# Modulation sums traced one group of products later in a two-layer trunk

## The chip, the core and the metric

The kernel runs on one core of a Trainium2 chip. The metric is the device time of one execution in microseconds (us); for the kernel before there are three runs, and their median counts.

## What is computed

A trunk of two layers acts on `x` (256 tokens x 1024). Each layer has three sub-layers, six in all, each wrapped in a modulation that depends on one conditioning vector `c`:

```python
def adaln_sublayer(x, m, f, ln_g, ln_b):
    shift, scale, gate = m[:, None, 0], m[:, None, 1], m[:, None, 2]
    y = f(x * (1 + scale) + shift)
    return layer_norm(DEEPNORM_ALPHA * x + (1 + gate) * y, ln_g, ln_b)
...
    cs = jax.nn.silu(c)
    for layer in range(DEPTH):
        mod = (cs @ mod_w[layer] + mod_b[layer]).reshape(bsz, N_SUB, 3, D_MODEL)
```

So each sub-layer needs three vectors of 1024 (scale and shift before `f`, the gate behind it), each `cs` (1024) times a 1024 x 1024 block of `mod_w`: 18 such products, 4 MB of weights each. `f` is a SwiGLU with d_ff 2816 (sub-layers 0, 2, 3, 5: ffn0 to ffn3), a hybrid of sparse attention and gated DeltaNet (sub-layer 1), and latent attention (MLA, sub-layer 4). All products are in float32.

## The kernel before

Large products are made of three passes on TensorE (`mm3`, L261; its instructions are L263 to L265), for which weights and activations are split into two parts: a cast on ACT (L258) and a subtraction on DVE or POOL (L259).

**An ffn** (L411) has 11 chunks of 256 columns. For chunk c, PE does the 96 gate and up products into four PSUM banks (pool tag `gu`, all four of them), then the 24 down products that belong to chunk c-1, then chunk c+1. ACT takes the SiLU of the gate (L548), DVE multiplies with the up part (`sg`, L551, the last reader of two banks) and splits the result (`h`). The last five down rows are kept for the end: there PE goes through the four accumulators one after the other with 15 products each. This is called the tail here; the epilogue (L381 and on: gate, residual, norm) follows it bank by bank. Down weights are loaded in tiles of 512 KB, pool tag `wd`, three slots.

**The modulation** is a background generator, `mod_gen` (L185). It does not use PE for the products: a tile of `mod_w` (128 x 1024, tag `wd` as well, so the same three slots) is multiplied on DVE with the column of `cs` that belongs to its partitions and added into `macc` (L218 for the first, L225 for the other seven tiles of a set). Behind the eighth, the 128 partitions are summed in `mod_sums` (L236): for scale and shift `mod_cols` transposes `macc` in eight pieces on PE (L138) into two banks, which DVE reduces (L139); for the gate `mod_gate` multiplies by a matrix of ones (L180, two products of 512 columns) and DVE adds the banks to `G` (L182). Sets come in the order scale, shift, gate of each sub-layer. There is one `macc`, so the first step of a set waits until the sums of the set before have read it.

**The order.** `pace` (L55) pulls as many steps as the progress of the sub-layer asks for; an ffn calls it twice in each chunk, traced behind the chunk's gate and up products and ahead of the down products. In the hybrid it is called by `beat` (L927) at fixed points, in the MLA once a head. `need` (L252) pulls a set to its end on demand, at the end of a sub-layer. The loads, all issued by SP in one order, the steps and the sums thus get their places; a scheduler then sets the final order of each engine from the traced one, and `behind` (L110) keeps an instruction from being ordered ahead of a given one on its own engine. PE, DVE and SP each work through their order strictly. The four places of a chunk:

```python
                        self.pace(max(0, i + 1 - skip) / (NT - 2 - skip))
                next(self.rest, None)
...
                if c:
                    for i in range(2 * c - 2, min(2 * c, NT - L)):
                        down(i, every)
```

Of the kernel before, what the change touches and what calls it, by code (L numbers as in the profile page):

```python
# [33 lines left out]
class Trunk:  # L34
# [20 lines left out]
    def pace(self, part):  # L55

        goal = self.base + math.ceil((self.goal - self.base) * min(part, 1.0))
        while self.count < goal:
            self.count += next(self.bg)
        if part > 1.0:  # L60
            self.need(self.si, 2)
            if self.si + 1 < len(self.subs):
                self.need(self.si + 1, 0)
# [121 lines left out]
    def mod_gen(self):  # L185
# [4 lines left out]
        ws, loaded, G, step = {}, 0, None, None  # L190
# [14 lines left out]
        for n, (si, i, k) in enumerate(todo):  # L205
            if k == 0:
                l, j = self.subs[si]
                off = (j * 3 + i) * D
                acc = self.tl(self.wp, [P, D], "G", bufs=2) if si == 0 and i < 2 else self.tl(self.wp, [P, D], "macc")
                if i == 2:  # L210
                    G = self.tl(self.wp, [P, D], "G", bufs=2)
# [12 lines left out]
            else:  # L224
                step = nc.vector.scalar_tensor_tensor(acc, w, c, acc, ALU.mult, ALU.add)  # L225
            yield 1
            if k < KD - 1:
                continue
            self.mod_sums(si, i, acc, G, step)
            self.mdone.add((si, i))  # L230
            yield 0
            if si == 0 and i == 1:
# [606 lines left out]
    def run(self, subs):  # L839
# [1 line left out]
        self.subs = subs  # L841
        self.mdone = set()
        self.count = 0
        self.marks, self.last_mm = [None], None
        self.left = None
        goals = (44, 64, 98, 132, 136, 144)
        self.setup()
# [690 lines left out]
```

## Time and profile before

| what | us |
|---|---|
| median of 3 runs | 1210.27 |
| lowest and highest run | 1207.26, 1211.66 |
| the profiled execution | 1209.47 |
| its span in the trace | 1207.7 |

The profile is of one execution; times below are from the start of its span. Sub-layers lie about so: ffn0 to 224 us, hybrid to 475, ffn1 to 674, ffn2 to 886, MLA to 1003, ffn3 to the end. A chunk of an ffn takes some 17 us. In a timeline row the first number is the start, the second the duration, then engine, line, operation, and in brackets what the engine waited for before it and how long. Matmuls overlap, so a product with a duration of 0.28 or 0.39 us starts 0.12 or 0.23 us behind the one before it.

### The profile page before, as it was taken

How to read it: one execution, taken by the hardware profiler on the slowest of the kernel's cores; microseconds unless marked ns; L12 is line 12 of the kernel's file. 1: busy time of each engine (PE TensorE's matmuls, PEld its weight loads, DVE VectorE, ACT ScalarE, POOL GpSimd, SP SyncE). 2: the span in 40 equal slices, each digit the busy share in tenths (PEclk: the TensorE clock that was granted, in tenths of full speed). 3: DMA queues.
4: the chain of work that ended last, by engine and by line, in shares of the span. 5: the costliest groups of instructions: out<-in, count | busy, mean ns of one | idle time of the engine just before them, and what ended most of it. 6: DMA issues, size and time to landing. Idle time of an engine off the chain costs nothing.

```text
span 1207.7 us, 19560 instructions
## 1 busy us (share of the span) xinstructions
PE 1131.0 (94%) x7703; PEld 1025.9 (85%) x7703; DVE 917.7 (76%) x1404; ACT 548.5 (45%) x963; POOL 259.4 (21%) x186
## 2 busy tenths in 40 slices
PE   4998999998899998999999999999989998999997
PEld 3887999788787887989999899898988877899995
DVE  6699777698986677878775889767789748866545
ACT  0645444456433445543543543434347656544430
POOL 0631000224731452320000342000122234300001
PEclk9998999999999999999999899999989999999999
DMA  9879998453310576789987488888733335885620
GB/s 354 266 252 342 299 327 299 139 179 119 97 36 5 188 270 218 238 293 320 311 298 248 134 284 283 270 278 298 250 122 102 139 105 190 294 253 185 211 71 35
DMA packets 155333, 259.74 MB, mean 215 GB/s; under 512 B 8813, under 2 KB 117354, under 8 KB 155242
## 3 DMA queue, kind: packets, MB, share of 16 engines
q1 hardware_dynamic: 155050, 258.45, 64.4%
q8 instruction: 60, 0.98, 0.3%
q14 instruction: 31, 0.25, 0.1%
q10 hardware_dynamic: 192, 0.05, 0.0%
HBM read 257.43 MB, written 1.05 MB: 214 GB/s over the span
## 4 chain that ended last, share of the span: by engine, by line
PE 51%; DVE 23%; DMA 13%; issue 5%; ACT 4%; POOL 3%; SPq 0%; POOLq 0%; DVEq 0%; ACTq 0%
PE gu L265 8%; PE gu L263 8%; PE gu L264 8%; PE acc L265 6%; PE acc L264 6%; PE acc L263 6%; DMA wd<-ffn_w_down 5%; DMA wd<-mod_w 4%; DVE macc L225 3%; DMA w<-ffn_w_up 2%; DVE g L259 2%; DVE x L383 1%; POOL hd L259 1%; DMA w<-mod_w 1%; DVE u L259 1%
## 5 line engine op out<-in xcount | busy, mean ns | idle before, releaser
L225 DVE SCALAR_TENSOR_TENSOR macc<-wd,csT,macc 128x1024 f32<-128x1024 f32 x112 | 171.5, 1531 | 28.6 <-DMA wd<-mod_w 28.0
L265 PE MATMUL gu<-uT,g 128*128 128x256 f32 x640 | 181.3, 283 | 1.6 <-DVE g L259 1.6
L263 PE MATMUL gu<-uT,g 128*128 128x256 f32 x640 | 181.2, 283 | 1.3 <-ACT sg L548 1.3
L265 PE MATMUL gu<-uT,u 128*128 128x256 f32 x640 | 181.3, 283 | 1.0 <-DVE u L259 1.0
L263 PE MATMUL gu<-uT,u 128*128 128x256 f32 x640 | 181.2, 283 | 0.0
L264 PE MATMUL gu<-uT,u 128*128 128x256 f32 x640 | 181.1, 283 | 0.0
L264 PE MATMUL gu<-uT,g 128*128 128x256 f32 x640 | 181.1, 283 | 0.0
L258 ACT CAST hd<-wd 128x1024 fp32r<-128x1024 f32 x88 | 92.3, 1049 | 136.8 <-DMA wd<-ffn_w_down 118.8
L263 PE MATMUL acc<-hd,h 128*128 128x512 f32 x352 | 141.5, 402 | 0.5 <-ACT h L258 0.5
L265 PE MATMUL acc<-hd,h 128*128 128x512 f32 x352 | 138.0, 392 | 1.8 <-DVE h L259 1.8
L264 PE MATMUL acc<-hd,h 128*128 128x512 f32 x352 | 138.1, 392 | 0.0
L259 DVE TENSOR_TENSOR g<-w,g 128x1024 fp32r<-128x1024 f32 x86 | 117.0, 1364 | 23.9 <-ACT g L258 23.8
L263 PEld LDWEIGHTS gu<-uT,g 128*128 128x128 f32 x640 | 122.7, 192 | 3.2 <-ACT sg L548 1.8
L265 PEld LDWEIGHTS gu<-uT,g 128*128 128x128 f32 x640 | 122.7, 192 | 2.2 <-DVE g L259 2.2
L264 PEld LDWEIGHTS gu<-uT,g 128*128 128x128 f32 x640 | 122.7, 192 | 1.4
L265 PEld LDWEIGHTS gu<-uT,u 128*128 128x128 f32 x640 | 122.9, 192 | 1.2 <-DVE u L259 1.2
L264 PEld LDWEIGHTS gu<-uT,u 128*128 128x128 f32 x640 | 122.9, 192 | 0.0
L263 PEld LDWEIGHTS gu<-uT,u 128*128 128x128 f32 x640 | 122.9, 192 | 0.0
L259 DVE TENSOR_TENSOR u<-w,u 128x1024 fp32r<-128x1024 f32 x81 | 106.6, 1321 | 20.1 <-ACT u L258 20.0
L259 POOL TENSOR_TENSOR hd<-wd,hd 128x1024 fp32r<-128x1024 f32 x32 | 89.6, 2806 | 137.9 <-ACT hd L258 137.9
L258 ACT CAST u<-w 128x1024 fp32r<-128x1024 f32 (+1 forms) x89 | 91.7, 1038 | 58.1 <-DMA w<-ffn_w_up 44.8
L259 POOL TENSOR_TENSOR hl<-w,hl 128x1024 fp32r<-128x1024 f32 x28 | 72.5, 2602 | 202.0 <-ACT hl L258 201.5
(403 smaller groups left out, 2477.6 us busy)
## 6 DMA issues: line engine op xcount, KB each, us to landing
wd<-mod_w SPq DMA_DIRECT2D x130, 512.0 KB, 4.8
wd<-ffn_w_down SPq DMA_DIRECT2D x88, 512.0 KB, 4.6
w<-ffn_w_gate SPq DMA_DIRECT2D x43, 1024.0 KB, 8.4
w<-ffn_w_up SPq DMA_DIRECT2D x43, 1024.0 KB, 6.3
w<-hyb_w_in SPq DMA_DIRECT2D x16, 1024.0 KB, 6.1
w<-mod_w SPq DMA_DIRECT2D x7, 1024.0 KB, 7.5
w<-hyb_w_out SPq DMA_DIRECT2D x4, 1024.0 KB, 5.0
w<-mla_w_out SPq DMA_DIRECT2D x4, 1024.0 KB, 5.1
```

The lines of the kernel that those rows point to most:

```text
L225: step = nc.vector.scalar_tensor_tensor(acc, w, c, acc, ALU.mult, ALU.add)
L258: i = self.nc.scalar.copy(hi, src)
L259: return i, (eng or self.nc.vector).tensor_tensor(out=lo, in0=src, in1=hi.bitcast(F32), op=ALU.subtract)
L263: nc.tensor.matmul(out, lh, rh, start=first, stop=False)
L264: nc.tensor.matmul(out, lh, rl, start=False, stop=False)
L265: self.last_mm = nc.tensor.matmul(out, ll, rh, start=False, stop=last)
L383: V.tensor_tensor(out=x[:, b, sl], in0=tmp, in1=x[:, b, sl], op=ALU.add)
```

## The change

Behind the eighth step of a set, `mod_gen` no longer traces the sums at once. It notes the last product that was traced (`last_mm`, set by every `mm3`), gives control back, and `pace` pulls nothing more as long as no further product has been traced. The next call of `pace` that finds a new one resumes: the sums are traced, ordered behind the last product on PE, and the steps that were due meanwhile follow at once. `need` does not look at the mark and pulls the sums directly. The first sets of sub-layer 0 are made before any product and keep their place. Tiles, pools, the split of work over engines and the goals stay as they were.

```diff
--- before.py
+++ after.py
@@ -55,7 +55,8 @@
     def pace(self, part):
 
         goal = self.base + math.ceil((self.goal - self.base) * min(part, 1.0))
-        while self.count < goal:
+        while self.count < goal and (self.held is None or self.held is not self.last_mm):
+            self.held = None
             self.count += next(self.bg)
         if part > 1.0:
             self.need(self.si, 2)
@@ -226,7 +227,14 @@
             yield 1
             if k < KD - 1:
                 continue
-            self.mod_sums(si, i, acc, G, step)
+            if self.last_mm is not None:
+
+                self.held = self.last_mm
+                yield 0
+                with self.behind(self.last_mm):
+                    self.mod_sums(si, i, acc, G, step)
+            else:
+                self.mod_sums(si, i, acc, G, step)
             self.mdone.add((si, i))
             yield 0
             if si == 0 and i == 1:
@@ -841,7 +849,7 @@
         self.subs = subs
         self.mdone = set()
         self.count = 0
-        self.marks, self.last_mm = [None], None
+        self.marks, self.last_mm, self.held = [None], None, None
         self.left = None
         goals = (44, 64, 98, 132, 136, 144)
         self.setup()
```

Lines behind the first hunk shift by 1, behind the second by 8 (L180 is L181, L225 is L226, L259 is L267, L551 is L559).

**PE, first gate sum (ffn0).** `macc_75` is the gate set of sub-layer 0, `gu_116` the last bank of chunk 3's products, `gu_138` that of chunk 4's in the new order. Before:

```order
L264 MATMUL gu_116_798<-uT_15_124,u_112_792 128x256
L265 MATMUL gu_116_798<-uT_15_124,u_112_792 128x256
L180 MATMUL gu_128_926<-macc_75_505,one_72 128x512
L180 MATMUL gu_129_929<-macc_75_505,one_72 128x512
L263 MATMUL acc_81_528<-hd_98_680,h_96_675 128x512
L264 MATMUL acc_81_528<-hd_98_680,h_96_675 128x512
L265 MATMUL acc_81_528<-hd_98_680,h_96_675 128x512
L263 MATMUL acc_82_532<-hd_98_680,h_96_675 128x512
```

Now:

```order
L272 MATMUL gu_138_999<-uT_15_124,u_134_993 128x256
L273 MATMUL gu_138_999<-uT_15_124,u_134_993 128x256
L181 MATMUL gu_143_1107<-macc_75_505,one_72 128x512
L181 MATMUL gu_144_1110<-macc_75_505,one_72 128x512
L655 MATMUL gu_154_1170<-ident_67,fr_1137 128x128
L271 MATMUL acc_81_528<-hd_120_903,h_118_898 128x512
L272 MATMUL acc_81_528<-hd_120_903,h_118_898 128x512
L273 MATMUL acc_81_528<-hd_120_903,h_118_898 128x512
```

The two products of the sum stand behind the products of the next chunk and ahead of the down products that follow those; with them comes a transpose of the position tables.

**SP, last heads of the hybrid.** `hyb_w_out` is the out projection's weight, the `wd` tiles belong to the scale set of sub-layer 2. Before:

```order
L892 DMA w8_698_4446<-hyb_w_out 128x2x1024
L892 DMA w8_718_4531<-hyb_w_out 128x2x1024
L198 DMA wd_630_4080<-mod_w 128x1024
L198 DMA wd_636_4103<-mod_w 128x1024
L198 DMA wd_637_4106<-mod_w 128x1024
L198 DMA wd_643_4129<-mod_w 128x1024
L198 DMA wd_649_4152<-mod_w 128x1024
L892 DMA w8_727_4586<-hyb_w_out 128x2x1024
L198 DMA wd_655_4215<-mod_w 128x1024
L198 DMA wd_656_4218<-mod_w 128x1024
```

Now:

```order
L900 DMA w8_698_4446<-hyb_w_out 128x2x1024
L900 DMA w8_718_4531<-hyb_w_out 128x2x1024
L900 DMA w8_727_4586<-hyb_w_out 128x2x1024
L199 DMA wd_650_4200<-mod_w 128x1024
L199 DMA wd_651_4203<-mod_w 128x1024
L199 DMA wd_652_4206<-mod_w 128x1024
L199 DMA wd_653_4209<-mod_w 128x1024
L199 DMA wd_654_4212<-mod_w 128x1024
L199 DMA wd_655_4215<-mod_w 128x1024
L199 DMA wd_656_4218<-mod_w 128x1024
```

The third `hyb_w_out` tile now stands ahead of the modulation tiles, which follow it in one row; before, five of them were ahead of it. On DVE the steps for which they are loaded (`macc_648`, behind the gate's two additions L183) now stand in one row as well, ahead of the reduces of their own sum:

```order
L183 SCALAR_TENSOR_TENSOR G_265_2067<-gu_646_4190,G_265_2067 128x512
L183 SCALAR_TENSOR_TENSOR G_265_2067<-gu_647_4193,G_265_2067 128x512
L219 TENSOR_SCALAR macc_648_4196<-wd_612_3982,csT_79 128x1024
L763 TENSOR_TENSOR PT_689_4415<-gu_619_4048,sums_620_4049 128x512
L226 SCALAR_TENSOR_TENSOR macc_648_4196<-wd_618_4045,csT_79,macc_648_4196 128x1024
L226 SCALAR_TENSOR_TENSOR macc_648_4196<-wd_649_4197,csT_79,macc_648_4196 128x1024
L226 SCALAR_TENSOR_TENSOR macc_648_4196<-wd_650_4200,csT_79,macc_648_4196 128x1024
L226 SCALAR_TENSOR_TENSOR macc_648_4196<-wd_651_4203,csT_79,macc_648_4196 128x1024
L226 SCALAR_TENSOR_TENSOR macc_648_4196<-wd_652_4206,csT_79,macc_648_4196 128x1024
L226 SCALAR_TENSOR_TENSOR macc_648_4196<-wd_653_4209,csT_79,macc_648_4196 128x1024
L226 SCALAR_TENSOR_TENSOR macc_648_4196<-wd_654_4212,csT_79,macc_648_4196 128x1024
L140 TENSOR_REDUCE ms_667_4341<-gu_668_4342 128x4
```

Before, the steps of this set stood one by one between the L736 of the heads (L744 in the new lines).

**DVE, end of ffn2.** `sg` and `h` are the last activations of the ffn, `hd` the last down weights, `big` weights of the MLA, `macc_1276` and `macc_1290` the shift set of the MLA. Before:

```order
L225 SCALAR_TENSOR_TENSOR macc_1276_8461<-wd_1423_9387,csT_79,macc_1276_8461 128x1024
L259 TENSOR_TENSOR h_1295_8625<-sg_1294_8622,h_1295_8625 128x256
L225 SCALAR_TENSOR_TENSOR macc_1276_8461<-wd_1424_9389,csT_79,macc_1276_8461 128x1024
L259 TENSOR_TENSOR hd_1317_8785<-wd_1316_8783,hd_1317_8785 128x1024
L225 SCALAR_TENSOR_TENSOR macc_1276_8461<-wd_1443_9476,csT_79,macc_1276_8461 128x1024
L551 TENSOR_TENSOR sg_1309_8764<-gu_1306_8665,sg_1309_8764 128x256
L259 TENSOR_TENSOR h_1310_8767<-sg_1309_8764,h_1310_8767 128x256
L551 TENSOR_TENSOR sg_1313_8775<-gu_1308_8667,sg_1313_8775 128x256
L259 TENSOR_TENSOR big_1319_8859<-w8_1318_8857,big_1319_8859 128x672
L259 TENSOR_TENSOR h_1315_8780<-sg_1313_8775,h_1315_8780 128x256
L259 TENSOR_TENSOR big_1321_8866<-w8_1320_8864,big_1321_8866 128x672
L381 SCALAR_TENSOR_TENSOR tmp_1328_8889<-acc_1110_7203,G_958_6178 128x512
```

Now:

```order
L267 TENSOR_TENSOR hd_1317_8785<-wd_1316_8783,hd_1317_8785 128x1024
L226 SCALAR_TENSOR_TENSOR macc_1290_8612<-wd_1422_9385,csT_79,macc_1290_8612 128x1024
L226 SCALAR_TENSOR_TENSOR macc_1290_8612<-wd_1423_9387,csT_79,macc_1290_8612 128x1024
L559 TENSOR_TENSOR sg_1313_8775<-gu_1308_8667,sg_1313_8775 128x256
L267 TENSOR_TENSOR big_1319_8859<-w8_1318_8857,big_1319_8859 128x672
L267 TENSOR_TENSOR big_1321_8866<-w8_1320_8864,big_1321_8866 128x672
L267 TENSOR_TENSOR h_1315_8780<-sg_1313_8775,h_1315_8780 128x256
L226 SCALAR_TENSOR_TENSOR macc_1290_8612<-wd_1424_9389,csT_79,macc_1290_8612 128x1024
L267 TENSOR_TENSOR big_1323_8873<-w8_1322_8871,big_1323_8873 128x672
L389 SCALAR_TENSOR_TENSOR tmp_1328_8889<-acc_1103_7181,G_976_6340 128x512
L226 SCALAR_TENSOR_TENSOR macc_1290_8612<-wd_1443_9476,csT_79,macc_1290_8612 128x1024
```

The steps of 1422 and 1423 stand behind the last `hd` and directly ahead of the last `sg`, and those of 1424 and 1443 behind the last `h`, among the epilogue's first operations; before, all four stood ahead of the last two `sg`. The end of ffn0 has the same shape.

## Rows read from the trace of the kernel before

**Rows 1.** The page: engines' busy time (us, share of span, instructions) and the chain that ended last.

```profile
PE 1131.0 (94%) x7703; PEld 1025.9 (85%) x7703; DVE 917.7 (76%) x1404; ACT 548.5 (45%) x963; POOL 259.4 (21%) x186
...
PE 51%; DVE 23%; DMA 13%; issue 5%; ACT 4%; POOL 3%; SPq 0%; POOLq 0%; DVEq 0%; ACTq 0%
```

**Rows 2.** The view of tile macc: the steps (minimum, median, maximum ns), and idle time of its users.

```profile
L225 DVE SCALAR_TENSOR_TENSOR macc<-wd,csT,macc x112: 1268/1279/3430, 60.3 to 1128.2; 128x1024 f32<-128x1024 f32 x112
...
  DVE macc L225: 7.2, 3
```

**Rows 3.** Waits of PE over the whole span: total us, times, longest us.

```profile
PE gu L138 <- DVE sg L551: 3.2, 2, 2.4
```

**Rows 4.** Timeline of PE: start us, duration, line, operation, in brackets the wait before it.

```profile
97.92 3.75 PE L180 MATMUL gu<-macc,one 128*128 128x512 f32 x4 [4.18 <-DVE macc L225]
...
102.75 0.39 PE L263 MATMUL acc<-hd,h 128*128 128x512 f32 x1
...
522.39 1.96 PE L180 MATMUL gu<-macc,one 128*128 128x512 f32 x4 [0.94 <-DVE macc L225]
...
524.88 0.40 PE L263 MATMUL acc<-hd,h 128*128 128x512 f32 x1
...
762.87 0.66 PE L138 MATMUL gu<-ident,macc 128*128 128x128 f32 x4 [2.43 <-DVE sg L551]
...
835.28 0.63 PE L138 MATMUL gu<-ident,macc 128*128 128x128 f32 x4 [2.08 <-DVE macc L225]
...
837.42 0.78 PE L263 MATMUL acc<-hd,h 128*128 128x512 f32 x1
...
840.09 0.40 PE L263 MATMUL acc<-hd,h 128*128 128x512 f32 x1
840.32 0.40 PE L264 MATMUL acc<-hd,h 128*128 128x512 f32 x1
```

**Rows 5.** Stretches of PE: span, us, PE busy (instructions), granted clock, DMA share, GB/s.

```profile
98.00:102.00 4.00, 4.00 (x6) 0.50 1.09 373
...
763.00:767.00 4.00, 4.00 (x20) 1.00 1.01 352
...
837.00:840.00 3.00, 3.00 (x10) 0.50 0.87 283
```

**Rows 6.** Timelines of DVE and PE at the start of ffn0's chunk 4.

```profile
100.33 1.23 DVE L259 TENSOR_TENSOR g<-w,g 128x1024 fp32r<-128x1024 f32 x1 [1.32 <-ACT g L258]
...
107.77 0.28 PE L265 MATMUL gu<-uT,g 128*128 128x256 f32 x1
```

**Rows 7.** The page: DMA issues (KB, median us to landing), and the cast of a down weight.

```profile
L258 ACT CAST hd<-wd 128x1024 fp32r<-128x1024 f32 x88 | 92.3, 1049 | 136.8 <-DMA wd<-ffn_w_down 118.8
...
wd<-mod_w SPq DMA_DIRECT2D x130, 512.0 KB, 4.8
```

**Rows 8.** Timeline of DVE at the end of ffn0.

```profile
213.54 3.97 DVE L225 SCALAR_TENSOR_TENSOR macc<-wd,csT,macc 128x1024 f32<-128x1024 f32 x3 [2.21 <-DMA wd<-mod_w]
...
220.60 0.42 DVE L551 TENSOR_TENSOR sg<-gu,sg 128x256 f32<-128x256 f32 x1 [1.86 <-PE gu L265]
```

**Rows 9.** Timelines of PE and SP in the hybrid's last heads.

```profile
427.51 0.28 PE L265 MATMUL acc<-uT,hl 128*128 128x256 f32 x1
427.63 1.03 PE L138 MATMUL gu<-ident,macc 128*128 128x128 f32 x8
...
406.31 11.43 SPq L198 DMA_DIRECT2D wd<-mod_w  x5
...
423.64 0.38 SPq L892 DMA_DIRECT2D w<-hyb_w_out  x1
```

**Rows 10.** Timeline of DVE at the end of ffn2.

```profile
862.70 1.29 DVE L225 SCALAR_TENSOR_TENSOR macc<-wd,csT,macc 128x1024 f32<-128x1024 f32 x1 [2.39 <-DMA wd<-mod_w]
...
870.63 0.42 DVE L551 TENSOR_TENSOR sg<-gu,sg 128x256 f32<-128x256 f32 x1
871.28 0.86 DVE L259 TENSOR_TENSOR big<-w,big 128x672 fp32r<-128x672 f32 x1 [0.22 <-ACT big L258]
```

## Prediction

> **What bounds the kernel.** I read the engines' busy time first, then the chain that ended last, the waits of PE, the timelines of PE, DVE and SP around the sums, and the granted clock in those stretches. PE is busy 94% of the span and DVE 76%; the chain lies 51% on PE, 23% on DVE and 13% on DMA [rows 1]. So a microsecond counts only where PE stands still, and the change can gain only from places where PE waits for a modulation sum. The view of tile `macc` finds three such waits, 7.2 us in all [rows 2]. In the waits of PE stand two more at the transposes, 3.2 us, for `sg` L551: the operation that frees a PSUM bank, not the sum's own data [rows 3].
>
> **What the waits cost, with the clock.** PE's timeline places the three at 97.92 (4.18 us, a gate sum), 522.39 (0.94, a gate sum) and 835.28 (2.08, transposes) [rows 4]. The first and the last cost more than their length. After the wait before 97.92 the granted clock stands at 0.50 over 98 to 102 us, the lower level of 1.2 GHz; PE had been idle for the 4.18 us before [rows 5]. The gate sum with three products takes 102.75 - 97.92 = 4.83 us there, against 524.88 - 522.39 = 2.49 us at the full clock: 2.34 us lost. After 835.28 the clock is 0.50 over 837 to 840: six products take 840.09 - 837.42 = 2.67 us, against 6 x 0.23 (840.09 to 840.32) = 1.38: 1.29 lost [rows 4, 5]. I book 2.3 and 1.2. The possible gain is 7.2 + 3.5 = 10.7 us.
>
> **How much of it goes.** In the new order each of these sums stands a whole chunk (some 17 us) behind its last step, so the step is done; no sum before was ever later than 4.2 us. But at 97.92 another wait is close behind. Chunk 4 begins on PE at 107.77 and its first weights were split from 100.33 on, when their load had just landed [rows 6]. Without the wait PE is there at 97.92 - 4.18 + 24 x 0.23 = 99.3. In the new order one 512 KB load less stands ahead of those weights, so I put the split's end at 100.2: 0.9 us of new wait. **Gain: 10.7 - 0.9 = 9.8 us** (ends 7 and 11). The sums themselves, about 2 us of PE for a gate [rows 4] and 1 us for eight transposes [rows 9], are moved and not added. The two bank waits (3.2 us) may go or come at any sum; I count 0, with -3 and +3 as ends.
>
> **What the pause costs inside an ffn.** The steps that were held back come in a bunch of up to six, 1.27 us each, behind the next chunk's products. The weights of the later chunks are split over 10 us before their use, so I count 0. If that cover were gone, the price would be the loads: 4.8 us to landing for each mod_w tile, through three slots that the down weights share [rows 2, 7]. What follows comes from there, at the three places where a bunch meets the end of a part.
>
> **End of ffn0.** The shift sum of sub-layer 1 moves from behind chunk 8 to behind chunk 9. Let X be PE's arrival there. The gate set's first step writes the same `macc`, so it ends near X + 3.4; two slots later the last down weight of the tail lands (4.8 us each, plus cast 1.05 [rows 7] and split 1.23 [rows 6]), split at X + 16.5; the next two steps end at X + 19.1 and now stand ahead of the last `sg` on DVE; `sg` and `h` bring the last `h` to X + 20.4. PE reaches the tail at X + 15.3 (transposes 1.0, 12 products of 0.23, 96 of 0.12) and that `h` four weight rows of 0.69 later, X + 18.1. Before, three steps in a row began at 213.54 and ended by 217.5, and `sg` at 220.60 waited for nothing but PE [rows 8]. New stall 2.3 us by this count, 1 if loads land sooner; I take 1.9, and 0.6 for the two steps that now stand in the epilogue. **+2.5** (0 to 4).
>
> **Hybrid.** The gate sum of sub-layer 1 moves from ahead of the attention to its last heads, some 20 us later, about 421 to 423 us of the trace before. The seven steps behind it then stand in a row on DVE. Before, five of their loads were issued from 406.31 on, and the transposes at 427.63, 0.12 us behind the product before them, waited for nothing [rows 9]. Now the loads stand in SP's queue behind the third hyb_w_out tile, which was issued at 423.64. The first of the seven ends near 425.3 and frees a slot; +4.8 is 430.1, +4.8 after the step that uses it 436.2, and the last of them 437.5. PE, less delayed, comes to the transposes 86 products of 0.12 us after the sum, about 433.5. That is 4 us by 4.8 a load; I take 3.5. A wait nearly as long cost 2.3 us of clock at 97.92, so I add 2.0. **+5.5** (1 to 8).
>
> The Trainium skill bears on this price: DMA: Bandwidth & Descriptors, sections "Latency and other measured facts" and "Measured (HBM→SBUF, 128 partitions, SWDGE, issued from GpSimd)", gives about 2 us of fixed cost and 341 GB/s for 1 MB. By that an estimate for a lone 512 KB load is 2 + 1.5 = 3.5 us, two loads in a row end 2.6 us sooner, the hybrid would cost about 1 us, and the sum below would come to about -2 us. The row says 4.8 [rows 7], and it decides.
>
> **End of ffn1.** Its gate sum moves behind chunk 10; the last down weight and `h` come just in time by the same count. **+0.5** (0 to 1.5).
>
> **End of ffn2.** The scale sum of the MLA moves behind chunk 9, as at ffn0, with one step more. On DVE two steps, then `sg`, two splits of `big` (0.86 each) and one `h` follow; that `h` comes at X + 22.2 by the same reckoning, needed at X + 18.1. Before, a step waited for its load until 862.70 (2.39 us) and all were done before the tail; `sg` came at 870.63 and the first `big` at 871.28 [rows 10]. The stall is 4.1 us with loads of 4.8, about 2 with quicker ones: I take 3. Two more steps (2.5 us) now lie beside the epilogue's first operations; most of that is beside PE's last three banks, so 0.8. **+3.8** (1 to 8 with a clock fall).
>
> MLA and ffn3 keep their order but for names: 0. **Sum: -9.8 + 2.5 + 5.5 + 0.5 + 3.8 = +2.5 us**, made against the profiled execution of 1209.47 us (span 1207.7): 1212.0. The median of the runs shown is 0.8 above it, so 1212.8, and I say 1213.
>
> **Rivals.** *A, the queues catch up (faster).* The waits and clock losses go, and the loads land early enough at all three ends. For it: 2.39 us of waiting for a load hid before the tail of ffn2 [rows 10]. Against: the slots allow three loads at a time, whatever DMA could do. It leaves -9.8 + 0.5 + 0.6 + 0.8 = -7.9: 1202.4 as a median, down to 1200.
>
> *B, each new stall also takes the clock (slower).* One mechanism, at the ends of ffn0 and ffn2: PE stops for `h` with products of three banks still to do, and those run at the lower level. It decides from about 2 us of stall on: the 2.43 us bank wait before 762.87 was not followed by a low clock (1.00 over 763 to 767), the 2.08 us before 835.28 was, with another short one behind it [rows 4, 5]. Price: 1.3 at ffn0 and 2.3 at ffn2, beside stalls at their full count (+0.4, +1.1) and the hybrid at 6.5: +2.5 + 6.1 = +8.6, or 1219. The Trainium skill, TensorE: Matmul & The Clock Gate, section "What's actually happening", says it so: "the default state is throttled, and activity releases the throttle." By that rule 1219 would be the forecast; the trace agrees at 97.92 and 835.28, not at 762.87.
>
> *C, the change doesn't do what it says.* The sums no longer wait for `macc` but as long for a bank of `gu`, all four of which the chunk holds. For it: the two waits for `sg` L551, 3.2 us [rows 3]. Against: they are two places of the whole trace. Clock kept or not, 7.2 us would come back: +9.7, 1220.
>
> **How the numbers follow.** 0.5%, 6 us, is about what a measurement of this kernel can tell from no change. The forecast with its neighbours between -6 and +6 gets 0.52. A gets 0.17, all of it counted as faster. B gets 0.23 and C 0.08, counted as slower. The range reaches from 1203, which takes in the near edge of A and the lower bounds of the three ends, to 1221, past B and C; I leave 0.12 below and 0.07 above. The forecast's own range is 1207 to 1216.
>
> **What would show it.** Right: no L180 or L138 waits for `macc` at 98, 522 and 835; a clock of 1.00 at 98 to 102; chunk 4 begins 5 to 6 us earlier; a new wait of PE for `macc` at the transposes near 430; waits for `h` in the tails of ffn0 and ffn2. Wrong: the tails run through (A); low clock slices in the tails (B); waits for `sg` L551 before most sums (C); or weights late in the middle of an ffn, for which I counted nothing.

## The result, and the profile after

| what | before | after |
|---|---|---|
| median of the runs, us | 1209.32 (4 runs, 1207.26 to 1211.66) | 1222.04 (4 runs, 1219.13 to 1223.30) |
| ratio, with its 95% interval | | 1.0101 [1.0074, 1.0128] |
| the profiled execution, and its span | 1209.47, 1207.7 | 1221.93, 1220.1 |

The change makes the kernel slower by 12.7 us, or 1.0%. The forecast was 1213, with a range to 1221.

The work is the same, so the page after shows little: the busy times are within 4 us of [rows 1], the modulation's loads land as before (4.7 us against 4.8 in [rows 7]), and PE has 57% of the chain instead of 51%.

```profile
PE 1134.6 (93%) x7703; PEld 1026.8 (84%) x7703; DVE 919.5 (75%) x1404; ACT 548.0 (45%) x963; POOL 258.3 (21%) x186
...
PE 57%; DVE 22%; DMA 10%; ACT 4%; issue 4%; POOL 2%; SPq 0%; POOLq 0%; DVEq 0%; ACTq 0%
...
wd<-mod_w SPq DMA_DIRECT2D x130, 512.0 KB, 4.7
```

The view of tile `macc` after, against [rows 2]: the three waits of 7.2 us are gone, and one of 7.8 us has come.

```profile
L226 DVE SCALAR_TENSOR_TENSOR macc<-wd,csT,macc x112: 1267/1279/3426, 60.8 to 1141.4; 128x1024 f32<-128x1024 f32 x112
...
  PE gu L139: 7.8, 1
```

To see where the time goes, the same instruction is looked up on PE's timeline in both traces. The last column is the forecast's sum of terms for the stretch.

| PE reaches | before | after | late by | of this stretch | forecast |
|---|---|---|---|---|---|
| chunk 3 of ffn0 | 80.80 | 81.80 | +1.0 | +1.0 | 0 |
| last group of products of ffn0 | 208.82 | 206.70 | -2.1 | -3.1 | -5.6 |
| transposes of `k` in the hybrid | 256.37 | 261.71 | +5.3 | +7.5 | +2.5 |
| first products of ffn1 | 491.09 | 505.28 | +14.2 | +8.9 | +5.5 |
| last group of ffn1 | 649.38 | 661.48 | +12.1 | -2.1 | -0.9 |
| first products of ffn2 | 694.28 | 710.01 | +15.7 | +3.6 | +0.5 |
| last group of ffn2 | 858.47 | 866.76 | +8.3 | -7.4 | -3.3 |
| first products of ffn3 | 1019.38 | 1031.83 | +12.4 | +4.2 | +3.8 |
| end of the span | 1207.7 | 1220.1 | +12.4 | 0.0 | 0 |

(In ffn1, 1.9 us of the two rows are the gate sum itself, which has moved from ahead of the last group to behind it.) The rows are of one execution each. The first one shows how far two executions can differ: nothing is changed ahead of chunk 3, and in the traces of all the runs below it begins between 80.1 and 82.4.

The timeline of PE after, at the places of [rows 4, 6, 9] and at the new waits:

```profile
100.62 0.39 PE L271 MATMUL gu<-uT,g 128*128 128x256 f32 x1 [0.41 <-ACT g L266]
101.88 0.39 PE L273 MATMUL gu<-uT,g 128*128 128x256 f32 x1 [0.76 <-DVE g L267]
113.25 1.88 PE L181 MATMUL gu<-macc,one 128*128 128x512 f32 x4
116.88 0.30 PE L655 MATMUL gu<-ident,fr 128*128 128x128 f32 x1 [1.75 <-ACT sg L556]
...
223.52 0.64 PE L271 MATMUL acc<-hd,h 128*128 128x512 f32 x1 [2.39 <-ACT h L266]
239.76 1.15 PE L290 MATMUL gu<-ident,x 128*128 128x128 f32 x8 [3.46 <-ACT x L413]
...
445.26 1.97 PE L139 MATMUL gu<-ident,macc 128*128 128x128 f32 x8 [7.80 <-DVE macc L226]
...
882.96 0.50 PE L271 MATMUL acc<-hd,h 128*128 128x512 f32 x1 [1.78 <-ACT h L266]
885.80 1.15 PE L273 MATMUL acc<-hd,h 128*128 128x512 f32 x2 [1.65 <-DVE h L267]
```

And stretches after (us; busy time and instructions of PE, PEld, DVE, ACT, POOL; granted clock; DMA share; GB/s), where [rows 5] had 0.50 at 98 and at 837:

```profile
98.00:102.00 4.00, 2.84 (x13) 1.92 (x12) 3.34 (x6) 2.57 (x4) 0.00 (x0) 1.00 1.08 380
...
222.00:226.00 4.00, 2.48 (x6) 1.98 (x7) 3.53 (x6) 2.94 (x4) 0.56 (x1) 0.71 0.70 234
...
242.00:246.00 4.00, 4.00 (x10) 3.13 (x11) 2.16 (x7) 3.33 (x10) 0.83 (x2) 0.50 0.96 332
445.00:449.00 4.00, 3.74 (x18) 3.75 (x19) 2.59 (x6) 0.62 (x2) 0.00 (x0) 0.50 0.88 285
...
837.00:840.00 3.00, 3.00 (x27) 3.00 (x26) 1.23 (x1) 2.27 (x3) 0.00 (x0) 1.00 0.72 255
...
884.00:888.00 4.00, 2.35 (x6) 1.75 (x6) 4.00 (x2) 0.87 (x2) 3.23 (x2) 0.74 0.88 301
```

What to see: the clock that the change was to keep at 98 and 837 is kept, at 1.00. It is lost instead at 222, 242, 445 and 884, each time behind a new wait of PE. At 242 the 0.50 is the lower of the two levels, 1.2 GHz, and the hybrid's first products run at it; before, the whole end of ffn0 had 1.00. From the last group of products to the transposes of `k`, before and then after:

```profile
208.82:256.37 47.55, 42.12 (x247) 35.91 (x245) 34.91 (x65) 22.75 (x45) 9.52 (x7) 1.00 0.47 147
```

```profile
206.70:261.71 55.01, 46.33 (x246) 39.17 (x244) 43.21 (x70) 24.81 (x47) 10.02 (x7) 0.91 0.56 169
```

Behind the 7.80 us at 445 stands DVE. Its steps after, in the hybrid's last heads:

```profile
428.02 2.60 DVE L226 SCALAR_TENSOR_TENSOR macc<-wd,csT,macc 128x1024 f32<-128x1024 f32 x2
432.57 4.74 DVE L226 SCALAR_TENSOR_TENSOR macc<-wd,csT,macc 128x1024 f32<-128x1024 f32 x2 [1.96 <-DMA wd<-mod_w]
434.03 11.17 DVE L226 SCALAR_TENSOR_TENSOR macc<-wd,csT,macc 128x1024 f32<-128x1024 f32 x4
```

POOL's splits of `hyb_w_out` beside them, and of the hybrid's first weights at the end of ffn0:

```profile
225.44 5.72 POOL L267 TENSOR_TENSOR hl<-w,hl 128x1024 fp32r<-128x1024 f32 x2 [128.40 <-ACT hl L266]
...
433.13 9.67 POOL L267 TENSOR_TENSOR hl<-w,hl 128x1024 fp32r<-128x1024 f32 x3 [0.25 <-ACT hl L266]
```

The two steps at 428 take 2.60 us, 1.3 each, with POOL idle for nearly all of it. Of the five from 432.57 on, the three that lie beside POOL's splits take 3.3 us each; the first and the last take 1.4 and 1.3. Only the first waited for its load. The trace of before had the same pair in the same place, with nobody waiting for it:

```profile
433.96 3.28 DVE L225 SCALAR_TENSOR_TENSOR macc<-wd,csT,macc 128x1024 f32<-128x1024 f32 x1
```

```profile
432.71 6.78 POOL L259 TENSOR_TENSOR hl<-w,hl 128x1024 fp32r<-128x1024 f32 x2 [1.08 <-ACT hl L258]
```

The Trainium skill says why this can be (SBUF — State Buffer, section "SBUF: two separate sides"): DVE and GpSimd share a pair of SBUF ports, and an operation of DVE with two inputs from SBUF and one of GpSimd that reads SBUF exclude each other, each for its whole length. The rows nearly agree: taken strictly in turn, a step of 1.28 and a split of 2.4 would make 3.7 us, and a pair takes 3.3.

At the end of ffn0 the same is seen on DVE after:

```profile
221.41 1.28 DVE L226 SCALAR_TENSOR_TENSOR macc<-wd,csT,macc 128x1024 f32<-128x1024 f32 x1 [2.19 <-DMA wd<-mod_w]
...
225.05 0.69 DVE L389 SCALAR_TENSOR_TENSOR tmp<-acc,G 128x512 f32<-128x512 f32 x1
225.66 3.26 DVE L226 SCALAR_TENSOR_TENSOR macc<-wd,csT,macc 128x1024 f32<-128x1024 f32 x1
228.84 2.88 DVE L391 TENSOR_TENSOR x<-tmp,x 128x512 f32<-128x512 f32 x1
```

A step that waited for its load holds back the last `sg`, so `h` comes late (PE's 2.39 us at 223.52). Another step then stands in the epilogue, in front of the residual add L391; both lie beside POOL's splits. The add takes 2.88 us; before, at the same place and beside a split too, it took 1.72, and 0.69 is its time with POOL idle. The first `x` that PE can transpose comes late (3.46 us at 239.76; before, PE waited 1.80 there). The same places before (DVE, then PE):

```profile
223.96 0.69 DVE L381 SCALAR_TENSOR_TENSOR tmp<-acc,G 128x512 f32<-128x512 f32 x1 [2.04 <-PE acc L265]
224.69 1.72 DVE L383 TENSOR_TENSOR x<-tmp,x 128x512 f32<-128x512 f32 x1
```

```profile
235.92 1.15 PE L282 MATMUL gu<-ident,x 128*128 128x128 f32 x8 [1.80 <-ACT x L405]
```

The epilogue's first operation on the accumulators (L381, now L389) divides the stretch. From PE's last group of products to it are 15.1 us before and 18.4 after; from it to the transposes of `x`, 12.0 and 14.7; from there to the transposes of `k`, 20.5 and 22.0. So of the 7.5 us lost here 3.2 come with the late `h`, 2.8 in the epilogue, and 1.5 behind it, with the lower clock at its start.

### The profile page after: what moved, and what is told of

It is laid out like the page before. It is cut to its first block, busy times and chain, and to the rows that moved or that the text cites. A ratio compares the mean times of both kernels' runs of the same rounds, so it can differ in the third digit from the quotient of the medians.

```text
span 1220.1 us, 19541 instructions
## 1 busy us (share of the span) xinstructions
PE 1134.6 (93%) x7703; PEld 1026.8 (84%) x7703; DVE 919.5 (75%) x1404; ACT 548.0 (45%) x963; POOL 258.3 (21%) x186
## 4 chain that ended last, share of the span: by engine, by line
PE 57%; DVE 22%; DMA 10%; ACT 4%; issue 4%; POOL 2%; SPq 0%; POOLq 0%; DVEq 0%; ACTq 0%
PE gu L272 9%; PE gu L271 9%; PE gu L273 9%; PE acc L273 7%; PE acc L271 7%; PE acc L272 6%; DMA wd<-ffn_w_down 4%; DVE macc L226 3%; DVE g L267 3%; DMA w<-ffn_w_up 2%; DVE u L267 1%; DVE x L391 1%; DMA w<-mod_w 1%; DMA wd<-mod_w 1%; DVE k L1043 1%
## 5 line engine op out<-in xcount | busy, mean ns | idle before, releaser
L226 DVE SCALAR_TENSOR_TENSOR macc<-wd,csT,macc 128x1024 f32<-128x1024 f32 x112 | 173.8, 1552 | 34.8 <-DMA wd<-mod_w 34.2
L267 DVE TENSOR_TENSOR g<-w,g 128x1024 fp32r<-128x1024 f32 x86 | 119.9, 1399 | 25.4 <-ACT g L266 24.9
L267 DVE TENSOR_TENSOR u<-w,u 128x1024 fp32r<-128x1024 f32 x81 | 104.0, 1290 | 35.5 <-ACT u L266 35.3
L267 POOL TENSOR_TENSOR hd<-wd,hd 128x1024 fp32r<-128x1024 f32 x32 | 88.1, 2760 | 155.2 <-ACT hd L266 155.2
L267 POOL TENSOR_TENSOR hl<-w,hl 128x1024 fp32r<-128x1024 f32 x28 | 73.8, 2646 | 208.7 <-ACT hl L266 208.2
```

The lines of the kernel that those rows point to most:

```text
L267: return i, (eng or self.nc.vector).tensor_tensor(out=lo, in0=src, in1=hi.bitcast(F32), op=ALU.subtract)
```

## The experiments

**The theory** from the comparison: the gain is there, but smaller in ffn0 than forecast, and two moves eat it: the gate sum of sub-layer 1 in the hybrid, and the sums of sub-layer 1 at the end of ffn0. The rivals: the steps held back delay weights everywhere, or the last chunks of each ffn are to blame. All kernels but one (e8) start from the changed one. Most of them hold fewer sums, by this one line:

```diff
-            if self.last_mm is not None:
+            if self.last_mm is not None and (si, i) in ((1, 2),):
```

(`si` is the sub-layer, `i` is 1 for scale, 0 for shift, 2 for gate.) Where the condition is a place instead of a set, a variable says which part of the program has called `pace`. The times, each against before on the same chip:

| run | held | median, us | before, us | ratio [95%] |
|---|---|---|---|---|
| e1 | all but in the hybrid | 1210.47 | 1208.35 | 1.0016 [1.0006, 1.0027] |
| e2 | only in the hybrid | 1217.74 | 1208.35 | 1.0075 [1.0052, 1.0098] |
| e3 | only in the ffn's chunks 0 to 7 | 1212.26 | 1208.35 | 1.0031 [1.0010, 1.0052] |
| e4 | all but in the ffn's chunks 8 and on | 1222.41 | 1208.35 | 1.0105 [1.0081, 1.0130] |
| e5 | all; `hyb_w_out` split on DVE | 1218.13 | 1209.54 | 1.0078 [1.0053, 1.0103] |
| e7 | as e1, ffn0 asks for 4 steps less | 1213.34 | 1209.54 | 1.0032 [1.0018, 1.0047] |
| e8 | none, ffn0 asks for 4 steps less | 1217.74 | 1209.54 | 1.0068 [1.0050, 1.0085] |
| e9 | as e1, hybrid's first weights split on DVE | 1225.28 | 1209.54 | 1.0118 [1.0090, 1.0145] |
| e10 | sums at 98, 522, 760 | 1207.86 | 1209.08 | 0.9997 [0.9983, 1.0011] |
| e11 | gate of sub-layer 0 (98) | 1206.70 | 1209.08 | 0.9991 [0.9975, 1.0007] |
| e12 | scale of sub-layer 1 | 1213.26 | 1209.08 | 1.0046 [1.0023, 1.0068] |
| e13 | scale of sub-layer 5 (835) | 1211.93 | 1209.08 | 1.0034 [1.0017, 1.0051] |
| e14 | all; no loads for the scale of sub-layer 2 | 1221.50 | 1208.21 | 1.0111 [1.0091, 1.0131] |
| e15 | as e14, `hyb_w_out` split on DVE | 1214.26 | 1208.21 | 1.0052 [1.0034, 1.0070] |
| e16 | gate of sub-layer 1 | 1219.60 | 1208.21 | 1.0100 [1.0083, 1.0116] |
| e17 | gate of 0, gate of 2 to gate of 4 | 1205.05 | 1208.21 | 0.9968 [0.9956, 0.9981] |
| e18 | shift of sub-layer 1 | 1213.78 | 1208.94 | 1.0032 [1.0019, 1.0045] |
| e19 | scale and shift of sub-layer 1 | 1215.01 | 1208.94 | 1.0052 [1.0032, 1.0071] |

**Which part of the program (e1 to e4).** The condition is the caller of `pace`:

```diff
+            if self.last_mm is not None and self.place[0] != "hybrid":
...
+            if self.last_mm is not None and self.place[0] == "hybrid":
...
+            if self.last_mm is not None and self.place[0] == "ffn" and self.place[1] < 8:
...
+            if self.last_mm is not None and not (self.place[0] == "ffn" and self.place[1] >= 8):
```

e1: 

> The change as it is, but in the hybrid the sums stay where they were before. Theory (the loss is local: about 8 us at the end of ffn0, 8 in the hybrid, 2 at the end of ffn1, 3 at the end of ffn2, against 11 gained in the ffns): the 7.8 us wait of PE at the transposes near 445 us goes, and the clock loss and the late steps behind it, so about 1213.5 us. Rival (a pause makes the shared load slots late everywhere, and the hybrid only shows it first): the wait moves to the next sums, and the time stays within 3 us of 1222.

e2: 

> The kernel before, with the sums held back in the hybrid alone. Local theory: 8 to 9 us over before, about 1218. Rival (diffuse lateness): under 3 us over before, since nothing was paused ahead of it.

e3: 

> The sums held back only in chunks 0 to 7 of an ffn, so neither in the hybrid nor where the bunch of steps meets the end of an ffn. Local theory: only gains are left, at the first gate sum (about 3 us net), at 522 (1 us) and at the bank wait at 760 (2.4 us): about 1203, faster than both kernels; the wait at 835 stays. Rival (diffuse lateness): not faster than before, 1209 or more.

e4: 

> The change, but in chunks 8 to 10 of an ffn the sums stay where they were. Local theory: the stalls in the tails go (8 + 2 + 3 us), the gain at 835 goes too (3 us), the loss in the hybrid stays: about 1212. Rival (the tails suffer from the load slots whatever chunk the sum is in): 1219 or more.

Without holding in the hybrid (e1) 10.6 of the 12.7 us are gone: 1210.47 - 1208.35 = 2.1 are left. Holding in the hybrid alone (e2) costs 9.4, with the same wait of 7.80 us for `macc`. So the hybrid carries most of it. e3 and e4 both came out slower than expected. In e3 the last chunks of ffn0 held nothing, and still PE reached the transposes of `k` 5.2 us late (261.61), from 2.5 early in ffn0; and giving up the late holding (e4) brought nothing. The pause in the late chunks is therefore not what alone loses the end of ffn0: in these two runs it is lost with sums held in the earlier chunks only.

**Which set in the hybrid (e16).** 

> Held: only the gate sum of sub-layer 1, the one that moves from ahead of the attention to its last heads. Theory (this one move puts the seven steps behind it in a row): a wait for macc near 440 us of 7 to 8 us, the first product of ffn1 later by 9 to 10 us than before, the run at 1216 to 1220. Rival (the holding of the sums of sub-layer 2 makes it): 1208 to 1211.

The gate sum of sub-layer 1 alone gives 11.4 us (1219.60 - 1208.21), and the wait of the change:

```profile
440.61 1.97 PE L139 MATMUL gu<-ident,macc 128*128 128x128 f32 x8 [7.81 <-DVE macc L226]
```

ffn1 begins 10.7 us late in the profiled execution, a little more than the 9 to 10 expected. One sum of sixteen is nearly as dear as the whole change.

**What makes the 7.8 us: loads, or the shared port (e5, e14, e15).** e5 puts POOL's splits of `hyb_w_out` on DVE; e14 takes the eight loads of the scale set behind that gate away (its steps then multiply the gate tile, so that scale is left out of the result); e15 does both.

```diff
-                op.ready(k, nc.gpsimd)
+                op.ready(k)
...
+            if (si, i) == (2, 1):
+                return
...
-            w, c = ws.pop((si, i, k)), self.cs[:, k : k + 1]
+            w, c = G if (si, i) == (2, 1) else ws.pop((si, i, k)), self.cs[:, k : k + 1]
```

e5: 

> The change, with the four splits of hyb_w_out in the hybrid's last heads moved from POOL to DVE. In the change three modulation steps in a row take 3.28 us there instead of 1.28, each beside one of POOL's splits. Port theory (a DVE operation with two SBUF operands and a POOL operation stand in each other's way): the steps come back to 1.28 us, the sum is done 2 to 4 us sooner though DVE gets 4.9 us of splits, PE's wait of 7.8 us shrinks to 4 to 5, and the time falls by some 3 us to about 1219. Load theory (the steps end late because their tiles land late): the steps still end where they did, the wait stays over 7 us, and the time rises with DVE's work, to 1222 or more.

e14: 

> The change, without the eight loads of the scale set of sub-layer 2 (4 MB): its steps multiply the gate tile instead, which is there, so this part of the modulation is left out of the result. The splits of hyb_w_out stay on POOL. If the steps beside POOL's splits (3.3 us instead of 1.28) alone carry the 7.8 us wait at the hybrid's transposes, it stays at 6 to 8 us, and the run at about 1220. If the loads alone carry it, it falls below 1.5 us and the run to 1211 to 1213. If both stand about equally far out, it falls by 0.5 to 3 us.

e15: 

> The same without the loads, and with the splits of hyb_w_out on DVE: neither the loads nor the shared port are left. Both theories: seven steps of 1.28 us and some splits of 1 us in a row are done before PE has its last products, so the wait for macc at the transposes is under 2 us and the run 1211 to 1214. If the wait stays above 4 us, it is the mere number of operations in a row on DVE, and neither of the two.

In e5 the steps are back at 1.3 us, but the last one waits for its load instead (DVE, then PE):

```profile
440.22 2.60 DVE L226 SCALAR_TENSOR_TENSOR macc<-wd,csT,macc 128x1024 f32<-128x1024 f32 x2
446.87 1.28 DVE L226 SCALAR_TENSOR_TENSOR macc<-wd,csT,macc 128x1024 f32<-128x1024 f32 x1 [2.92 <-DMA wd<-mod_w]
```

```profile
448.21 1.97 PE L139 MATMUL gu<-ident,macc 128*128 128x128 f32 x8 [7.54 <-DVE macc L226]
```

That load has another place than in the change. With the splits on DVE, the fourth `hyb_w_out` tile is issued among the steps' loads; in the change it stands behind them all (SP in e5, then in the change):

```profile
438.00 0.38 SPq L900 DMA_DIRECT2D w<-hyb_w_out  x1
439.20 9.31 SPq L199 DMA_DIRECT2D wd<-mod_w  x4
```

```profile
437.34 8.22 SPq L199 DMA_DIRECT2D wd<-mod_w  x4
445.61 0.43 SPq L900 DMA_DIRECT2D w<-hyb_w_out  x1
```

The load that e5's last step waits for is the one issued at 439.20, behind that tile, and it took 7.6 us to land. The one of the change's last step was issued at 437.34 and took 3.5; it had been there for 3 us when the step began at 443.91.

In e14 there is no load to wait for; five steps in a row take 14.54 us, the four beside POOL's splits 3.3 each and the last 1.3 (DVE, then PE):

```profile
431.96 14.54 DVE L228 SCALAR_TENSOR_TENSOR macc<-G,csT,macc 128x1024 f32<-128x1024 f32 x5
```

```profile
446.56 1.97 PE L139 MATMUL gu<-ident,macc 128*128 128x128 f32 x8 [8.31 <-DVE macc L228]
```

In e15, with neither (one of the four splits on DVE, then PE):

```profile
428.26 1.22 DVE L269 TENSOR_TENSOR hl<-w,hl 128x1024 fp32r<-128x1024 f32 x1
```

```profile
439.05 1.21 PE L139 MATMUL gu<-ident,macc 128*128 128x128 f32 x8 [4.38 <-DVE macc L228]
```

| wait of PE for `macc`, us | loads as they are | loads taken away |
|---|---|---|
| splits on POOL | 7.80 (the change) | 8.31 (e14) |
| splits on DVE | 7.54 (e5, in another order of loads) | 4.38 (e15) |

Without loads, the splits on POOL alone hold the wait at 8.31 us (e14). Taking them off POOL then lowers it by 3.9 us, although DVE now has their work as well (e15). So steps and splits side by side are enough for the wait, and in the change it is they that end last: after 432.57 no step waited more than 0.1 us for anything but the step before it. The runs show that the two slow each other; that a shared port is the reason, no run here tests apart. That the loads alone would make a wait as long is not shown either, since e5's last load stood behind a tile that the change has behind the loads. An estimate from the change's own rows: with steps of 1.28 us, the last load could be issued at 434.03 + 1.28 = 435.3; with the 3.5 to 4.8 us that these loads take to land, the last step would end at 440.1 to 441.4, where PE, waiting from 437.46 on, got the sum at 445.26. Some 2.6 to 3.9 of the 7.8 us would be left, about the 4 that the forecast counted for the loads (it took 3.5).

e15's 4.38 us were expected under 2, and the expectation reads more than 4 as the mere number of operations in a row on DVE. Four of these are splits of 1.22 us, 4.9 us in all, that e15 itself puts there. Without them the row would end, by estimate, about when PE arrives; no run left them out. The median of e15 is 7 us below that of e14. In the two traces 5.5 us of this lie between the transposes of `k` and ffn1, and 3.6 had come before, in a part where the two don't differ.

**The end of ffn0 (e12, e18, e19).** The scale sum, the shift sum, or both sums of sub-layer 1 are held, nothing else.

e12: 

> Held: only the scale sum of sub-layer 1 (at 153 us before). Theory: there was no wait to gain there, and the pause puts the last steps of ffn0 into its tail: a wait of PE for h near 225 and an epilogue longer by some us, 1213 to 1216. Rival (it is the first gate sum that does it): within 1.5 us of before, 1208 to 1211.

e18: 

> Held: only the shift sum of sub-layer 1 (at 188 us before), the sum that the forecast's step on the end of ffn0 names. Forecast's step: a late h in the tail and two steps in the epilogue, +2.5 us (0 to 4): 1210 to 1213. Rival (it is holding it together with the scale sum ahead of it, which leaves two bunches in one chunk): within 1 us of before.

e19: 

> Held: the scale and the shift sum of sub-layer 1, all others where they were. The first product of ffn1 was 6.3 us late by the end of ffn0 in the run with no holding in the hybrid, and 3.0 late when the scale sum alone was held. Theory (the loss at ffn0's end comes from these two and is nearly whole here): first product of ffn1 later by 5 to 7 us, a wait for h in the tail and a longer one for x in the epilogue, 1212 to 1216. Rival (it takes the first gate sum too): later by 3 to 4 us, 1210 to 1213.

By the medians each of the two alone loses: 4.2 us (e12), 4.8 us (e18), and both 6.1 us (e19); their losses don't add up. e12's ten executions spread from 1209.96 to 1223.07 us, and the profiled one, at 1210.04, is near the fastest. In it PE waits 0.94 us for `h` in the tail, no step stands in the epilogue, and the wait for `x` is the 1.80 us of before. So where the 4.2 us of e12 lie is not shown. e18, whose one moved sum is the one in the forecast's step, shows the way most plainly. DVE:

```profile
224.98 0.68 DVE L389 SCALAR_TENSOR_TENSOR tmp<-acc,G 128x512 f32<-128x512 f32 x1
225.58 3.31 DVE L226 SCALAR_TENSOR_TENSOR macc<-wd,csT,macc 128x1024 f32<-128x1024 f32 x1
228.81 2.88 DVE L391 TENSOR_TENSOR x<-tmp,x 128x512 f32<-128x512 f32 x1
```

PE, and its clock behind the second wait:

```profile
223.46 0.50 PE L271 MATMUL acc<-hd,h 128*128 128x512 f32 x1 [1.29 <-ACT h L266]
...
239.73 1.97 PE L290 MATMUL gu<-ident,x 128*128 128x128 f32 x8 [5.06 <-ACT x L413]
```

```profile
238.00:242.00 4.00, 2.01 (x9) 1.61 (x9) 3.96 (x12) 2.63 (x7) 0.00 (x0) 0.50 0.76 154
```

The late `h` is the smaller part: PE waits 1.29 us for it, and the epilogue's first operation comes 17.2 us behind the last group of products, 2.1 more than before. The larger is the epilogue, 14.8 us instead of 12.0: PE waits 5.06 us for `x`, where it waited 1.80 before, and goes on at the lower clock. PE reaches the transposes of `k` 4.2 us late (260.52). The profiled execution of e19 was the slowest of its ten, so its places are not used as a sum.

**Is it the number of steps at the end of ffn0 (e7, e8)?** ffn0 is capped at 40 of its 44 steps, with the holding of e1 and in the kernel before:

```diff
+        if self.si == 0:
+            goal = min(goal, 40)
```

e7: 

> No holding back in the hybrid (as in the first run of this study), and ffn0 stops at 40 steps, the last that the hybrid needs at its start, so that the four steps of the gate set leave ffn0's tail and go to the hybrid. Tail theory (the 6 us that are lost between ffn0's last chunk and ffn1 come from modulation steps among the last splits and the epilogue): they go, about 1204.5 us, faster than before. Rival (the late h is an order that the scheduler finds anyway, or the four steps cost as much in the hybrid): 1210 as without the cap.

e8: 

> The kernel before with the same cap at 40 steps in ffn0. Tail theory: before had no stall there, so nothing is gained, 1208 within 2 us. If it is as fast as the run with the change's holding and the cap, the gain is the cap's and not the holding's.

The steps don't leave the end of ffn0. In e8's trace the shift sum of sub-layer 1 now comes at 219.96, at the end of the sub-layer, and six steps of the gate set follow it on DVE between 221.57 and 235.20, in and around the epilogue's operations. With no sum held, PE waits 7.05 us for `x`, and the run is 8.2 us slower. So modulation work in the epilogue is enough for such a loss, however it comes there. With the cap, holding (e7) is 4.4 us better than not holding (e8). **e9**, which put the splits beside the epilogue on DVE, was to free the port there: 

> No holding back in the hybrid, and POOL's two splits of the hybrid's first weights, which run beside the epilogue of ffn0, on DVE. Port theory: the modulation step of 3.3 us and the residual's addition of 2.9 us in that epilogue fall to 1.3 and 0.7, against 2.4 us of splits more for DVE; PE's wait for x of 5.1 us falls to 2 to 3, about 1208. Rival (POOL's work is not the cause): the two keep their durations and the time goes up by the 2.4 us, 1212.5.

It was slower by 1.2%, but the order of DVE changed in many places, with new waits for `h`, `uT` and `hl`; it says nothing on the port, and that part of the epilogue's loss is read from the rows, not tested.

**What one sum gains alone (e10, e11, e13).**

e11: 

> Held: only the gate sum of sub-layer 0. Theory: chunk 4 begins about 5 us earlier, that is kept to the end of ffn0 with no wait for h there, and the run ends at about 1204 to 1206. Rival: the gain is gone at the hybrid's first product, 1209 to 1211, although neither sum of sub-layer 1 was held.

e13: 

> Held: only the scale sum of sub-layer 5 (at 835 us before). Theory: the waits at 835 go (about -4.5 with the clock) and come back in the tail of ffn2 (waits for h, some 5 us with the clock): 1208 to 1211, no difference that can be measured. Rival (the tail's loss is that of the steps in the change's later chunks alone, whatever is held): 1204 to 1205.

e10: 

> Held: only the gate sum of sub-layer 0 (at 97.92 us before), the gate sum of sub-layer 2 (522) and the shift sum of sub-layer 4 (760); all others stand where they stood before. Theory (a sum that waits gains what its wait and the clock behind it cost; what the change loses at the ends of the ffn and in the hybrid comes from holding the others): 97.92 gives back about 5 (4.18 + 2.34 less a short wait at chunk 4), 522 gives 0.9, 760 its 2.4 us bank wait less what appears elsewhere: 1201 to 1203 us against 1209, faster by 0.5 to 0.7%. Rival (holding the first gate sum alone already puts the steps of the tail of ffn0 late, because every step behind it moves): about 1208, with a wait of PE for h at the end of ffn0.

e11: from chunk 3 to the last group of ffn0, PE gains 3.2 us (0.5 late, then 2.8 early), as the change does. In the profiled execution 1.5 of them go between there and ffn1 and 2.2 more at the end of ffn2; why, no run here tells. The median gains 2.4 us, less than can be told from nothing: the theory's 3 to 5 did not come out, and the rival's loss of all of it in the hybrid did not either. e13: holding the sum at 835 gains 4.8 us (1.2 late at 821, 3.6 early at the last group of ffn2), and from there to ffn3 5.7 are lost again (2.2 late in ffn3). PE in the tail of ffn2:

```profile
871.89 0.50 PE L271 MATMUL acc<-hd,h 128*128 128x512 f32 x1 [2.56 <-ACT h L266]
874.75 1.22 PE L273 MATMUL acc<-hd,h 128*128 128x512 f32 x2 [1.12 <-DVE h L267]
```

The clock over 872 to 876 is 0.54. The median is 2.9 us slower, a little beyond the theory's bound. e10 missed: with the sum at 522 held and the next one, of sub-layer 3, not, that next one waited:

```profile
559.66 1.94 PE L139 MATMUL gu<-ident,macc 128*128 128x128 f32 x8 [3.14 <-DVE macc L226]
```

PE was 2.7 us early ahead of it and 3.4 late behind. In this run, then, the pause put its steps off, and the next sum, not given the same slack, paid for them.

**A version that beats both (e17).** From that: hold the sums that wait, and all that follow them up to a place where the steps have slack again; leave those of sub-layer 1, those in the hybrid and the one ahead of ffn2's tail.

```diff
+            if self.last_mm is not None and (si, i) in ((0, 2), (2, 2), (3, 1), (3, 0), (3, 2), (4, 1), (4, 0), (4, 2)):
```

> Held: the gate sum of sub-layer 0 and, from the gate sum of sub-layer 2 on, all up to the gate sum of sub-layer 4; not those of sub-layer 1, nor those in the hybrid, nor the scale sum of sub-layer 5. Theory (holding one sum and not the next one moves the wait to the next, as at 559 us in the run with three sums held; holding them in a row keeps the gain): ffn1 begins about 1.3 us early, the gate sum of sub-layer 2 gains 2.9 more, the wait for the bank at 760 gains 2, so 1204 to 1206, ratio 0.996 to 0.998. Rival (what one sum gains is paid at the next part's end, whatever is held): 1208 to 1211.

1205.05 us, ratio 0.9968 [0.9956, 0.9981]: 3.2 us faster than before and, by the two ratios, 1.3% faster than the change. ffn1 begins on time, its last group is 2.8 us early, and no sum in ffn1 waits. The one wait of PE for `macc` that is left is that of the sum at 835, which isn't held:

```profile
840.26 1.09 PE L139 MATMUL gu<-ident,macc 128*128 128x128 f32 x8 [1.66 <-DVE macc L226]
```

## Why the prediction was wrong

The direction of every term was right, and the sum was not: +2.5 forecast, +12.4 in the trace. Four of the moves were run alone, and by the medians each came out dearer than its terms: the gate sum of sub-layer 0, -2.4 us against -5.6 (e11; its interval reaches past zero); the shift sum of sub-layer 1, +4.8 against +2.5 with ends 0 to 4 (e18); the gate sum of sub-layer 1, +11.4 against +5.5 with ends 1 to 8 (e16); the scale sum of sub-layer 5, +2.9 against -3.3 + 3.8 (e13). Two terms lie outside their own ends, and both have DVE's steps beside POOL's splits at a price that was never counted. By the forecast's own steps:

- **Gain at 97.92** (-5.6 with the clock): the wait and the low clock went, and the 0.9 us of new waits for chunk 4's weights came as 0.41 + 0.76. But the sum in its new place brings a wait for a bank (1.75 us at 116.88), which the forecast had at zero with 3 us either way. -3.1 is left. Rival C named this; it decided here alone.
- **"I count 0" inside the ffn** nearly held: PE's waits for the split `g` grew from 1.6 us in 2 places to 3.2 in 4, and 0.76 of that is the one at 101.88.
- **End of ffn0** (+2.5, ends 0 to 4): +7.5, the largest miss. The late `h` is 3.2 of it, with a wait of 2.39 us, against 1.9 taken (2.3 counted). The failed step is "0.6 for the two steps that now stand in the epilogue": the epilogue is 2.8 us longer. One of the two steps stands in front of the residual add, beside POOL's split, at 3.3 us, and the add behind it takes 2.9 (e18 has the same rows). That the port costs this is read from the rows, since e9 did not settle it. For the 1.5 us behind the epilogue, at the lower clock, the forecast had no term. And the shift sum is not the only cause: the scale sum held alone loses 4.2 us by the median (e12).
- **Hybrid** (+5.5, ends 1 to 8): +8.9. The place, the waiting instruction and its releaser were right. The failed step is the time of the seven steps in a row, taken as a chain of loads with 1.27 us a step. Beside POOL's splits a step takes 3.3 us, and this ended last in the change; it makes a wait of 8.31 us with no loads at all (e14), and 3.9 less with the splits off POOL (e15). The stall was 7.8 us against the 3.5 taken for loads, a count that no run refutes, and the clock fell as booked.
- The evidence was in the rows quoted: [rows 2] gives the steps as 1268/1279/3430 ns, and I used the first two numbers and did not ask what the third was.
- **End of ffn1** (+0.5): about +1.7 without the moved sum; PE waits 1.85 us for the split `hd` at 679.69.
- **Inside ffn2** (-3.3): -7.4; the bank waits at 762.87 and 836.66 (2.43 and 0.75 us), counted at 0, nearly went as well (0.4 us of them is left). That this offset part of the losses was luck: the forecast had no reason for it.
- **End of ffn2** (+3.8): +4.2, with waits of 1.78 and 1.65 us. (The forecast called the scale sum there, and the shift set behind it, those of the MLA; they are of sub-layer 5, ffn3. Places and numbers are not touched.)
- **The price of a load**, where the Trainium skill (DMA: Bandwidth & Descriptors, section "Latency and other measured facts") spoke against the row: whichever is right, a run without these loads still waited 8.31 us (e14), so the choice between 3.5 and 4.8 us could not decide the hybrid's term.
- **Rivals.** A, in which the queues catch up, is excluded by all three ends. B foresaw that new stalls take the clock. It did at ffn0 and in part at ffn2, but B's bound of about 2 us of stall does not come out of the rows (1.78 and 1.65 us took it, 2.43 did not), and its 1219 has only 6.5 us for the hybrid. C, whose 1220 was the nearest number given, did not happen but for one bank, so that nearness is luck. None of them had the shared port.

## What to carry to other kernels

When work is put off, ask at every place where the bunch now lands who stands behind it, and with which engine it runs side by side there: the same DVE step cost 1.3 us alone and 3.3 us beside a split on POOL, and that was harmless only as long as nobody waited. A minimum, median and maximum that lie far apart in one row are a question to be answered before that row is used as a price. Give slack to the instructions that wait, one by one, and to those that inherit their delay (e17), and not to all of a kind: of the sixteen sums here one alone cost nine tenths of what the whole change did.

## What was not expected of the hardware

- A step on DVE, 128 x 1024 with two inputs from SBUF, takes 1.28 us alone and 3.2 to 3.4 where all of it lies beside splits on POOL, whose own time grows from 2.4 to as much as 3.5 us; a residual add of 128 x 512 grows from 0.69 to 1.72 (before) and 2.88 (after).
- In these rows the clock does not follow from the length of a wait alone: behind the 2.43 us before 762.87 it stayed at 1.00 [rows 4, 5], and with waits of 1.78 and 1.65 us at 883 to 886 it was 0.74 on average over 884 to 888.
